# A fused two-block transformer kernel: the first and last Strassen quads get a fifth accumulator, the rms diagonal moves to ScalarE, and constant matmuls run first

## The chip, the cores and the metric

The kernel runs on one core of one Trainium2 chip. The metric is the device time of one launch in microseconds (us); several runs are made and the median is given. The core has TensorE (PE, the matrix engine), VectorE (DVE), ScalarE (ACT), GpSimd (POOL) and SyncE (SP); here POOL and SP also start the DMA transfers that bring weights from HBM.

## The reference, cut to what matters

The input is one sequence of 512 positions, 1024 channels wide, in float32. Two blocks follow each other:

```
h = x + mix(rms_norm(x))                       # gated linear attention and latent attention
h = h + square(relu(rms_norm(h) @ w_up)) @ w_down            # mlp, 4096 wide
h = h + (p @ w_ple_proj) * sigmoid(rms_norm(h) @ w_gate + b) # ple
...
for i in range(2):                              # second block
    x = x + (pool_mixer if i == 0 else chunk_attention)(rms_norm(x))
    n = rms_norm(x)
    a = causal_dwconv3(n @ w_gate)              # 2816 wide
    x = x + (silu(a) * (n @ w_val)) @ w_out     # ffn
```

`rms_norm` divides each position by the root of its mean square. All weights are used once, so they stream from HBM through the core. The change touches the mlp and the two ffn stages (their up-projections), the row scales of the norms, and the first microseconds.

## The kernel before, in words

**Layout.** Activations lie transposed: a tile is 128 channels by 512 positions. Every float32 matrix product is made of three matmuls on a high and a low part of each operand (`mm3`: high by high, high by low, low by high), so every weight tile `ws` is split into `wh` (on ACT, a copy that rounds) and `wl` (on DVE, the difference), two halves of 128x512 each.

**Stages and quads.** The stages are mix, mlp, ple, pool, ffn0, att, ffn1. The up-projections of mlp and the ffns use a Strassen-Winograd scheme: after a first group of plain tiles (`first_tiles`, accumulators `pf`), the output tiles are taken in fours, a *quad*, with 7 products in place of 8. `PHASES` lists the seven: b11, b21, n3, n2, n1, b22, t4. In the list of orders they are numbers 0 to 6 in the order of `PHASES`. Each is 24 matmuls into one accumulator bank: b11, n2, n1 and b22 all go into `pq0`, one on top of the other; b21 into `pq1`, n3 into `pq2`, t4 into `pq3`. Intermediate states of `pq0` are wanted, so `quad_step` copies it on ACT after b11 (to `c1`), after n2 (to `u2`) and after n1 (to `u4`); the next phase into `pq0` waits for that copy. DVE then forms the four results (`c1`+`pq1`, `u2`, `u4`, `pq0`), and `quad_row` multiplies them by the row scale `R` into tiles `qr`. `finish` turns these into the inputs of the down-projection: in ffn the convolution and silu (`fb`, on ACT and DVE), the product, and the split into `yh` (ACT) and `yl` (DVE). The down-projection's accumulators are `pdn`; DVE adds them into the residual `x`.

**Weight sums.** n3, n2 and b22 use sums of weight blocks. One tile, called "sum", is loaded by SP with block 0; POOL then adds blocks to it with accumulating DMAs: block 2 at once (for n3), block 3 after n3's split (for n2), block 1 after n2's split (for b22). `LOADS` says when in the stream of work units each tile is asked for. The tile called "low", for n1, takes one such DMA too.

**Row scale.** `stats` sums the squares with PE (`pst`), takes the power on POOL (`r`), multiplies the identity by `r` on DVE (`dg`, four tiles of 128x128), sums the columns on PE (`psr`), and copies that on ACT to `R`.

**What sets the order.** The program is written out by a planner, and the scheduling is manual: the order in which the planner issues instructions is the order in each engine's stream. Tasks (`spawn`) have priorities; `drive` issues the best task whose inputs are ready on a modelled clock (`Pace.note`), and `splitter` keeps the weight splits up to `lazy` units ahead of their use, with `NW` = 4 buffers each for `wh` and `wl`.

In the trace nearly every instruction carries line 147, the helper that records and issues; the functions themselves are `stats` (line 497), `mix_start` (554), `units_quads` (1242), `quads` (1297) and `quad_step` (1342).

Of the kernel before, what the change touches and what calls it, by code (L numbers as in the profile page):

```python
# [12 lines left out]
AF = mybir.ActivationFunctionType  # L13
OP = mybir.AluOpType
# [36 lines left out]
PHASES = (("b11", 0, True, "a11"), ("b21", 1, True, "a12"), ("n3", 2, True, "sum"), ("n2", 0, False, "sum"),  # L51
          ("n1", 0, False, "low"), ("b22", 0, False, "sum"), ("t4", 3, True, "a22"))

ORDERS = (0, 1, 2, 3, 6, 4, 5), (2, 0, 1, 3, 6, 4, 5)

LOADS = (("sum", 0, -3, (2,)), ("a11", 0, 1, ()), ("a12", 1, 2, ()), ("low", 2, 2.5, (3,)), ("a22", 3, 4, ()))

# [119 lines left out]
class Quad:  # L177


    def __init__(self, src):  # L180
        self.src, self.tile = src, {}


class Block:
# [86 lines left out]
    def plan_loads(self):  # L271

        self.loads, known = [], set()
        for n, u in enumerate(self.units):
            if not isinstance(u[0], str):
                self.loads.append((n, n, u[0], u[1], None, ()))
            elif u[1] not in known:
                known.add(u[1])
                for name, block, at, more in LOADS:
                    self.loads.append((n + at, u[1], u[1].src[block], 1024, name, more))  # L280
        self.loads.sort(key=lambda e: e[0])

# [214 lines left out]
    def stats(self, norm, row):  # L497
        nc = self.nc
        late = 0.0 if norm.gain == self.GAIN["mix"] else self.LATE
        self.pace.ready[norm.acc.tensor.name] += late  # L500
        yield self.room(7)
        yield [norm.acc]
        ps = self.bank("pst")
        for j in range(NT):
            nc.tensor.matmul(ps[:, j:j + 1], norm.acc[:, j * P:(j + 1) * P], self.ones[:, :1], start=True, stop=True,
                             skip_group_check=True)
        norm.acc = None
        norm.ms = self.small("ms", NT)
        nc.vector.tensor_scalar(norm.ms, ps[:, :NT], 1.0 / DM, EPS, op0=OP.mult, op1=OP.add)
        self.free()  # L510
        norm.r = self.power("r", norm.ms, NT)
        if not row:
            return
        yield [norm.r]
        dg = self.slot("dg")
        for j in range(NT):
            nc.vector.tensor_scalar(dg[:, j * P:(j + 1) * P], self.ident, norm.r[:, j:j + 1], None, op0=OP.mult)
        self.pace.ready[dg.tensor.name] += late
        yield self.room(7)
        yield [dg]  # L520
# [33 lines left out]
    def mix_start(self, norm):  # L554
# [9 lines left out]
        def split(d):  # L564
            norm.xs[d] = self.hilo("xs", xin[d], scale=self.col(norm.gain, d))

        load(0)
        load(1)
        self.load_units(1)
# [671 lines left out]
    @staticmethod  # L1241
    def units_quads(plain, src, downs, sizes):

        quads, units, order, wait = [Quad(src[4 * i:4 * i + 4]) for i in range(sum(sizes) - 1)], [], [], []
        q, left = -1, sum(sizes)
        for g, n in enumerate(sizes):
            for i in range(n):
                left -= 1
                if q < 0:
                    order.append((q, 0))  # L1250
                    units += plain
                else:
                    most = 0 if q == 0 else -(-len(wait) // (n - i)) if left else len(wait) - 2
                    for at, ph in enumerate(ORDERS[q > 0]):
                        order.append((q, ph))
                        units.append(("quad", quads[q], ph))
                        for _ in range(((5, 2, 6, 3) if i else (5, 6, 4, 3))[:min(most, len(wait))].count(at)):
                            order.append(wait[0][:2])
                            units.append(wait.pop(0)[2])
                q += 1  # L1260
            for w in wait:
                order.append(w[:2])
                units.append(w[2])
            wait = [("down", (g, u), x) for u, x in enumerate(downs[g])]
        for w in wait:
            order.append(w[:2])
            units.append(w[2])
        return units, order

    def first_tiles(self, norm, take, acts):  # L1270

# [22 lines left out]
            if w % 2:  # L1294
                self.spawn(self.finish(acts, rows, w // 2, 0), -1)

    def quads(self, norm, order, sizes, last, after, take, finish, late=None):


        group = []  # L1300
# [5 lines left out]
        for what, i in order:  # L1306
# [4 lines left out]
            if what < 0:  # L1311
                yield from self.first_tiles(norm, take, acts[0])
                continue
            block, acc, first, _ = PHASES[i]
            if quad is None:
                if late is not None and what == sum(sizes) - 2:
                    self.spawn(late(), 5)
                ps, quad = [None] * 4, {"norm": norm, "take": take, "rows": [None, None], "left": [2, 2],
                                        "acts": acts[group[what + 1]], "at": what + 1 - group.index(group[what + 1])}
            yield from self.unit(8, P)  # L1320
            unit = self.got
# [13 lines left out]
                             first and k == 0 and w == 0, k == 3)  # L1335
            self.used(ps[acc])
            if i != 2:
                self.spawn(self.quad_step(i, ps, quad), -3)
            if i == 5:
                ps = quad = None  # L1340

    def quad_step(self, i, ps, quad):

        s, v = self.nc.scalar, self.nc.vector
        yield [ps[PHASES[i][1]]]
        if i in (0, 3, 4):
            name = {0: "c1", 3: "u2", 4: "u4"}[i]
            t = self.slot(name)
# [2 lines left out]
        if i == 3:  # L1351
            yield [t, ps[2]]
            v.tensor_sub(t, ps[2], t)
        elif i == 1:
            yield lambda: "c1" in quad
            t = quad["c1"]
            yield [t]
            v.tensor_add(t, ps[1], t)
            self.free()
            self.spawn(self.quad_row(quad, 0, 0, t), -2)  # L1360
        elif i == 4:
            yield [t, ps[2]]
# [41 lines left out]
    def units_mlp(self):  # L1404
        a = self.a
        at, downs = 0, []
        for n in QG1:
            downs.append([(a["w_down"][at + i], 1024) for i in range(4 * n)])
            at += 4 * n
        units, self.order["mlp"] = self.units_quads([(a["w_up0"][i], 1024) for i in range(4)],  # L1410
                                                    [a["w_up"][i] for i in range(FF1 // P - 4)], downs, QG1)
        return units

    def mlp(self, norm, after):
# [13 lines left out]
                self.sub(l, z, h.bitcast(F32))  # L1428
                acts[4 * i + 2 * r + w] = h, l

        yield from self.quads(norm, self.order["mlp"], QG1, 4, after, take, finish, self.load_p)
        norm.blocks = None

    def product(self, norm, name, finish):
# [141 lines left out]
    def units_ffn(self, L):  # L1576
        a = self.a
        at, downs = 0, []
        for n in QG2:
            downs.append([(a[f"w_fo{L}"][at + i], 1024) for i in range(2 * n)])  # L1580
            at += 2 * n
        units, self.order["ffn", L] = self.units_quads([(a[f"w_f{L}_0"][i], 1024) for i in range(4)],
                                                       [a[f"w_f{L}"][i] for i in range(2 * FF2 // P - 4)], downs, QG2)
        return units

    def ffn(self, L, norm, after):
# [27 lines left out]
                acts[2 * i + w] = self.hilo("y", y)  # L1614

        gates = {}
        yield from self.quads(norm, self.order["ffn", L], QG2, 2, after, self.mul, finish)
        norm.blocks = None


# [344 lines left out]
```

## Time and profile before

| | |
|---|---|
| median of 3 runs | 1682.46 us (1681.58 to 1685.93) |
| the profiled execution's own time | 1680.26 us |
| its span, first to last instruction | 1678.5 us |
| PE busy | 1626.3 us, 97% of the span |
| DVE busy | 1262.8 us, 75% |
| ACT busy | 882.0 us, 53% |
| POOL busy | 282.4 us, 17% |
| mean granted TensorE clock | 0.992 |

How to read it: the span is what the trace covers; the time of the execution holds 1.8 us more. The profiled execution is 2.2 us under the median of the three runs. A PE that is busy 97% of the span leaves about 52 us of gaps; what a change of this kind can win or lose lies in these gaps and in the stretches where the clock stands below 1.

### The profile page before, as it was taken

To read this page: it belongs to the slowest core of one execution; us is meant where nothing else is said; L and a number is where in the kernel's file an instruction comes from. 1 tells how busy PE (TensorE), PEld (TensorE's weight loads), DVE (VectorE), ACT (ScalarE), POOL (GpSimd) and SP (SyncE) were. 2 spreads that over 40 slices of the span, in tenths; PEclk is the share of its full clock that TensorE was granted. 3 is DMA by queue.
4 is the path that set the end of the run, shared out by engine and by line. 5 is a ranking of instruction groups with operands and counts; after the bars stand their busy time and mean duration, and the time that the engine had idled before them with its cause. 6 is when DMAs were issued, how large, how long until landed. Compare 5 with 4: busy or idle time off the path is not lost. (4 is left out here: it accounts for less than half of the span.)

```text
span 1678.5 us, 27783 instructions
## 1 busy us (share of the span) xinstructions
PE 1626.3 (97%) x10640; PEld 1459.2 (87%) x10640; DVE 1262.8 (75%) x2444; ACT 882.0 (53%) x1714; POOL 282.4 (17%) x312
## 2 busy tenths in 40 slices
PE   8999999999999999989999999999999989999998
PEld 6878778799999988879999998999998879999997
DVE  6986778766666667878787778576678988787776
ACT  6746446544444455845454444476656654454542
POOL 3441302000000013211111100322222211011100
PEclk9999999999999999989999999999999999999999
DMA  7101233566566423267777763322122367776751
GB/s 266 63 26 39 77 100 90 150 163 163 163 164 174 140 101 116 63 164 179 185 191 186 190 163 126 114 76 89 64 92 73 103 161 189 188 189 183 180 156 60
DMA packets 66390, 224.85 MB, mean 134 GB/s; under 512 B 7617, under 2 KB 9554, under 8 KB 66258
## 3 DMA queue, kind: packets, MB, share of 16 engines
q1 hardware_dynamic: 50706, 166.46, 28.1%
q0 software_dynamic: 15552, 56.63, 19.1%
q8 instruction: 83, 1.36, 0.3%
q14 instruction: 49, 0.40, 0.1%
HBM read 220.96 MB, written 2.10 MB: 133 GB/s over the span
## 5 line engine op out<-in xcount | busy, mean ns | idle before, releaser
L147 ACT ACTIVATE wh<-ws 128x512 fp32r<-128x512 f32 x690 | 392.8, 621 | 257.9 <-PE pdn L147 121.5
L147 DVE TENSOR_TENSOR wl<-ws,wh 128x512 fp32r<-128x512 f32 x665 | 437.0, 699 | 91.0 <-ACT wh L147 90.8
L147 PE MATMUL pq<-xsh,wh 128*128 128x256 f32 x864 | 246.6, 285 | 10.1 <-ACT u L147 10.1
L147 PE MATMUL pq<-xsl,wh 128*128 128x256 f32 x864 | 245.8, 285 | 0.0
L147 PE MATMUL pq<-xsh,wl 128*128 128x256 f32 x864 | 245.8, 284 | 0.0
L147 PEld LDWEIGHTS pq<-xsh,wh 128*128 128x128 f32 x864 | 167.1, 193 | 12.9 <-ACT u L147 11.7
L147 DVE TENSOR_TENSOR x<-x,pdn 128x512 f32<-128x512 f32 x177 | 119.8, 680 | 74.8 <-PE pdn L147 74.7
L147 POOL DMA_DIRECT2D ws<-in_w_f x80 | 70.7, 936 | 593.6 <-DVE wl L147 309.2
L147 PEld LDWEIGHTS pq<-xsl,wh 128*128 128x128 f32 x864 | 167.2, 193 | 1.2
L147 PEld LDWEIGHTS pq<-xsh,wl 128*128 128x128 f32 x864 | 167.0, 193 | 0.0
L147 PE MATMUL pdn<-yl,wh 128*128 128x512 f32 x352 | 138.7, 394 | 3.0 <-DVE yl L147 3.0
L147 PE MATMUL pdn<-yh,wh 128*128 128x512 f32 x352 | 138.2, 392 | 1.1 <-ACT yh L147 1.1
L147 PE MATMUL pdn<-yh,wl 128*128 128x512 f32 x352 | 137.5, 391 | 0.0
L147 PE MATMUL pq<-xch,wh 128*128 128x256 f32 x432 | 126.0, 292 | 7.1 <-ACT wh L147 5.3
L147 PE MATMUL pq<-xch,wl 128*128 128x256 f32 x432 | 124.5, 288 | 1.0 <-DVE wl L147 1.0
L147 PE MATMUL pq<-xcl,wh 128*128 128x256 f32 x432 | 123.9, 287 | 0.0
L147 PE MATMUL paq<-wh,xsh 128*128 128x256 f32 x384 | 111.3, 290 | 1.8 <-DVE akk L147 1.2
L147 PE MATMUL paq<-wl,xsh 128*128 128x256 f32 x384 | 108.6, 283 | 0.0
L147 PE MATMUL paq<-wh,xsl 128*128 128x256 f32 x384 | 108.5, 283 | 0.0
L147 PE MATMUL pdn<-hh,wh 128*128 128x512 f32 x256 | 99.9, 390 | 0.0
L147 PE MATMUL pdn<-hl,wh 128*128 128x512 f32 x256 | 99.9, 390 | 0.0
L147 PE MATMUL pdn<-hh,wl 128*128 128x512 f32 x256 | 99.6, 389 | 0.0
(328 smaller groups left out, 3914.8 us busy)
## 6 DMA issues: line engine op xcount, KB each, us to landing
ws<-in_w_f SPq DMA_DIRECT2D x108, 512.0 KB, 4.3
ws<-in_w_f POOLq DMA_DIRECT2D x80, 512.0 KB, 5.4
ws<-in_w_fo SPq DMA_DIRECT2D x44, 512.0 KB, 5.1
ws<-in_w_up SPq DMA_DIRECT2D x39, 512.0 KB, 3.3
ws<-in_w_down SPq DMA_DIRECT2D x32, 512.0 KB, 3.7
ws<-in_w_up POOLq DMA_DIRECT2D x28, 512.0 KB, 5.6
ws<-in_w_out SPq DMA_DIRECT2D x8, 512.0 KB, 3.2
ws<-in_w_gate SPq DMA_DIRECT2D x8, 512.0 KB, 3.2
```

The lines of the kernel that those rows point to most:

```text
L147: return call(*args, **kw)
```

## The change

- The three orders are now called FIRST (0,1,2,3,6,4,5: the order the first quad of a stage had before), MOST (2,0,1,3,6,4,5: as before) and LAST (2,0,1,3,5,4,6: new, with b22 ahead of n1 and t4 at the end). LAST is used for the last quad of ffn0 and of ffn1. mlp's last quad keeps MOST.
- In quads with FIRST (mlp, ffn0, ffn1) or LAST (ffn0, ffn1), b22 starts a fifth accumulator `pq4` of its own; DVE adds it to `u4`, and the fourth result gets its own slot `c22`.
- In a first quad the "sum" tile is asked for five units ahead of its use, not three.
- The diagonal `dg` is made on ACT instead of DVE in all stages but mix, and the planner is told to expect it later (1.5 times the allowance), so it places `psr` later.
- Ahead of everything, 18 matmuls of constant tiles, `warm`, 128x128 in float32.

```diff
-ORDERS = (0, 1, 2, 3, 6, 4, 5), (2, 0, 1, 3, 6, 4, 5)
+FIRST, MOST, LAST = (0, 1, 2, 3, 6, 4, 5), (2, 0, 1, 3, 6, 4, 5), (2, 0, 1, 3, 5, 4, 6)
...
                 for name, block, at, more in LOADS:
+                    at = -5 if u[1].order == FIRST and name == "sum" else at
...
-            nc.vector.tensor_scalar(dg[:, j * P:(j + 1) * P], self.ident, norm.r[:, j:j + 1], None, op0=OP.mult)
-        self.pace.ready[dg.tensor.name] += late
+            if late:
+                nc.scalar.activation(dg[:, j * P:(j + 1) * P], self.ident, AF.Copy, scale=norm.r[:, j:j + 1])
+            else:
+                nc.vector.tensor_scalar(dg[:, j * P:(j + 1) * P], self.ident, norm.r[:, j:j + 1], None, op0=OP.mult)
+        self.pace.ready[dg.tensor.name] += 1.5 * late
...
+        ps = self.bank("warm")
+        for _ in range(18):
+            self.tc.nc.tensor.matmul(ps[:, :P], self.ones, self.ones, start=True, stop=True)
+        self.free()
         load(0)
...
-                    for at, ph in enumerate(ORDERS[q > 0]):
+                    quads[q].order = FIRST if q == 0 else MOST if left or most > 0 else LAST
+                    for at, ph in enumerate(quads[q].order):
...
+            own = quads[what].order != MOST
+            if i == 5 and own:
+                acc, first = 4, True
...
-            if i == 5:
+            if i == quads[what].order[-1]:
                 ps = quad = None
...
         elif i == 4:
             yield [t, ps[2]]
-            v.tensor_sub(t, ps[2], t)
+            c = self.slot("c22") if own else t
+            v.tensor_sub(c, ps[2], t)
+            self.free(2 if own else 1)
+            quad["c22"] = True
+            self.spawn(self.quad_row(quad, 1, 1, c), -2)
+        elif i == 5 and own:
+            yield lambda: "c22" in quad
+            t = quad["u4"]
+            yield [t, ps[4]]
+            v.tensor_add(t, ps[4], t)
             self.free()
-            self.spawn(self.quad_row(quad, 1, 1, t), -2)
+            self.spawn(self.quad_row(quad, 0, 1, t), -2)
```

**How the order moves, 1: ACT in the last quad of ffn0.** `wh_10592` before and `wh_10617` now are n2's split, `wh_10705` and `wh_10654` are b22's (both read the "sum" tile, `ws_10138` and `ws_10163`), `c1` and `u2` are the copies of `pq0`. Before:

```order
L147 ACTIVATE wh_10592<-ws_10138 128x512 x2
L147 ACTIVATE yh_10602<-qr_10380 128x512
L147 ACTIVATE wh_10629<-ws_10371 128x512 x2
L147 ACTIVATE c1_10640<-pq0_10591 128x512
L147 ACTIVATE yh_10642<-qr_10381 128x512
L147 ACTIVATE wh_10667<-ws_10336 128x512 x2
L147 ACTIVATE wh_10705<-ws_10138 128x512 x2
L147 ACTIVATE u2_10716<-pq0_10591 128x512
```

Now:

```order
L148 ACTIVATE wh_10617<-ws_10163 128x512 x2
L148 ACTIVATE yh_10627<-qr_10405 128x512
L148 ACTIVATE wh_10654<-ws_10163 128x512 x2
L148 ACTIVATE c1_10665<-pq0_10616 128x512
L148 ACTIVATE yh_10667<-qr_10406 128x512
L148 ACTIVATE wh_10692<-ws_10361 128x512 x2
L148 ACTIVATE wh_10730<-ws_10396 128x512 x2
L148 ACTIVATE u2_10741<-pq0_10616 128x512
```

b22's split, which waits for the third addition to the "sum" tile, stood behind the `c1` copy and now stands ahead of it. In the last quad of ffn1 the same rows move in the same way.

**How the order moves, 2: DVE in the first quad of ffn0.** `dg` is the diagonal, `c1` the first result, `qr` from `pf` the plain tiles' scaling by `R`, `qr` from `c1` the first result's; the three pairs of `wl` are the splits of n2, t4 and n1. Before:

```order
L147 TENSOR_SCALAR dg_7484<-ident_65,r_7431 128x128 x4
L147 TENSOR_TENSOR c1_7492<-pq1_7483,c1_7492 128x512
L147 TENSOR_TENSOR qr_7439<-pf_7204,R_7525 128x512
L147 TENSOR_TENSOR qr_7440<-pf_7205,R_7525 128x512
L147 TENSOR_TENSOR qr_7441<-pf_7206,R_7525 128x512
L147 TENSOR_TENSOR qr_7442<-pf_7207,R_7525 128x512
L147 TENSOR_TENSOR qr_7540<-c1_7492,R_7525 128x256
L147 TENSOR_TENSOR qr_7541<-c1_7492,R_7525 128x256
L147 TENSOR_TENSOR wl_7554<-ws_6713,wh_7553 128x512 x2
L147 TENSOR_TENSOR wl_7561<-ws_7031,wh_7560 128x512 x2
L147 TENSOR_TENSOR wl_7569<-ws_6954,wh_7568 128x512 x2
```

Now:

```order
L148 TENSOR_TENSOR c1_7514<-pq1_7505,c1_7514 128x512
L148 TENSOR_TENSOR wl_7568<-ws_6653,wh_7567 128x512 x2
L148 TENSOR_TENSOR wl_7575<-ws_7053,wh_7574 128x512 x2
L148 TENSOR_TENSOR wl_7583<-ws_6976,wh_7582 128x512 x2
L148 TENSOR_TENSOR qr_7461<-pf_7226,R_7559 128x512
L148 TENSOR_TENSOR qr_7462<-pf_7227,R_7559 128x512
L148 TENSOR_TENSOR qr_7463<-pf_7228,R_7559 128x512
L148 TENSOR_TENSOR qr_7464<-pf_7229,R_7559 128x512
L148 TENSOR_TENSOR qr_7594<-c1_7514,R_7559 128x256
L148 TENSOR_TENSOR qr_7595<-c1_7514,R_7559 128x256
L148 TENSOR_TENSOR u2_7626<-pq2_7537,u2_7626 128x512
```

The diagonal has left DVE, and the six scalings now follow the six weight splits that they preceded. The first quad of ffn1 shows the same exchange.

## Rows read from the trace of the kernel before

**Rows 1.** Waits of PE: engine, who released it: total us, times, longest.

```profile
PE pq L147 <- ACT u L147: 10.1, 8, 2.1
...
PE pq L147 <- ACT wh L147: 5.3, 3, 3.3
```

**Rows 2.** Timeline of the start, PE and DVE: start, us, engine, operation, [idle before].

```profile
7.84 0.80 PE L147 MATMUL pl<-xsh,wh 128*128 128x512 f32 x1 [7.84 <-ACT wh L147]
...
11.85 0.45 PE L147 MATMUL pl<-xsh,wh 128*128 128x512 f32 x1
...
9.03 4.06 DVE L147 SCALAR_TENSOR_TENSOR xsl<-xin,cols,xsh 128x512 fp32r<-128x512 f32 x6
```

**Rows 3.** Timeline of PE, first quad of mlp: n1, then b22.

```profile
306.65 0.38 PE L147 MATMUL pq<-xsh,wh 128*128 128x256 f32 x1 [1.98 <-ACT u L147]
...
310.47 0.38 PE L147 MATMUL pq<-xsh,wh 128*128 128x256 f32 x1 [0.69 <-ACT u L147]
```

**Rows 4.** Timeline of PE, first quad of ffn0: psr, n2, n1, b22, down-projection.

```profile
721.65 1.78 PE L147 MATMUL psr<-dg,ones 128*128 128x512 f32 x2 [2.21 <-DVE dg L147]
...
727.90 0.39 PE L147 MATMUL pq<-xch,wh 128*128 128x256 f32 x1 [1.44 <-ACT wh L147]
...
736.70 0.39 PE L147 MATMUL pq<-xsh,wh 128*128 128x256 f32 x1 [0.78 <-ACT u L147]
...
741.90 0.39 PE L147 MATMUL pq<-xsh,wh 128*128 128x256 f32 x1 [2.07 <-ACT u L147]
...
755.71 0.40 PE L147 MATMUL pdn<-yh,wh 128*128 128x512 f32 x1
```

**Rows 5.** Busy time by stretch, ffn0: PE, PEld, DVE, ACT, POOL, granted clock, DMA.

```profile
741.90:745.60 3.70, 3.70 (x19) 3.70 (x20) 3.67 (x8) 1.67 (x3) 0.53 (x1) 0.57 0.95 164
```

**Rows 6.** Timeline of POOL, ACT, DVE, first quad of ffn0.

```profile
720.26 1.32 POOL L147 DMA_DIRECT2D ws<-in_w_f  x1
...
727.22 3.23 ACT L147 ACTIVATE wh<-ws 128x512 fp32r<-128x512 f32 x6 [3.16 <-DMA ws<-in_w_f]
...
724.09 2.48 DVE L147 TENSOR_TENSOR qr<-pf,R 128x512 f32<-128x512 f32 x4 [1.99 <-ACT R L147]
726.49 0.75 DVE L147 TENSOR_TENSOR qr<-c,R 128x256 f32<-128x256 f32 x2
727.88 3.70 DVE L147 TENSOR_TENSOR wl<-ws,wh 128x512 fp32r<-128x512 f32 x6 [0.64 <-ACT wh L147]
731.50 1.53 DVE L147 SCALAR_TENSOR_TENSOR fb<-qr,cols,fb 128x511 f32<-128x511 f32 x2
```

**Rows 7.** Timeline of PE, first quad of ffn1: n2, n1, b22, down-projection.

```profile
1349.27 0.39 PE L147 MATMUL pq<-xch,wh 128*128 128x256 f32 x1 [3.29 <-ACT wh L147]
...
1358.37 0.39 PE L147 MATMUL pq<-xsh,wh 128*128 128x256 f32 x1 [1.10 <-ACT u L147]
...
1363.58 0.56 PE L147 MATMUL pq<-xsh,wh 128*128 128x256 f32 x1 [2.08 <-ACT u L147]
...
1377.40 0.40 PE L147 MATMUL pdn<-yh,wh 128*128 128x512 f32 x1
```

**Rows 8.** Timeline of POOL, ACT, PE, last quad of ffn0: b22's addition, c1, b22's split, n2.

```profile
1011.87 0.86 POOL L147 DMA_DIRECT2D ws<-in_w_f  x1 [12.30 <-DVE wl L147]
...
1013.33 0.60 ACT L147 ACTIVATE c<-pq 128x512 f32<-128x512 f32 x1 [1.26 <-PE pq L147]
...
1017.09 1.15 ACT L147 ACTIVATE wh<-ws 128x512 fp32r<-128x512 f32 x2 [1.60 <-DMA ws<-in_w_f]
...
1016.01 0.28 PE L147 MATMUL pq<-xch,wh 128*128 128x256 f32 x1
```

**Rows 9.** Timeline of PE, end of ffn0: b22, down-projection.

```profile
1025.50 0.38 PE L147 MATMUL pq<-xsh,wh 128*128 128x256 f32 x1 [0.69 <-ACT u L147]
...
1028.47 0.40 PE L147 MATMUL pdn<-yh,wh 128*128 128x512 f32 x1
...
1043.17 0.80 PE L147 MATMUL pdn<-yl,wh 128*128 128x512 f32 x1 [1.84 <-DVE yl L147]
```

More of the change, by code (lines that the diff above doesn't have):

```diff
@@ L180, in __init__ @@
     def __init__(self, src):
-        self.src, self.tile = src, {}
+        self.src, self.tile, self.order = src, {}, MOST
 class Block:
@@ L1267, in units_quads @@
             units.append(w[2])
-        return units, order
+        return units, order, quads
     def first_tiles(self, norm, take, acts):
@@ L1295, in first_out, with quads @@
                 self.spawn(self.finish(acts, rows, w // 2, 0), -1)
-    def quads(self, norm, order, sizes, last, after, take, finish, late=None):
+    def quads(self, norm, order, quads, sizes, last, after, take, finish, late=None):
         group = []
@@ L1317, in quads @@
                     self.spawn(late(), 5)
-                ps, quad = [None] * 4, {"norm": norm, "take": take, "rows": [None, None], "left": [2, 2],
+                ps, quad = [None] * 5, {"norm": norm, "take": take, "rows": [None, None], "left": [2, 2],
                                         "acts": acts[group[what + 1]], "at": what + 1 - group.index(group[what + 1])}
@@ L1337, in quads, with quad_step @@
             if i != 2:
-                self.spawn(self.quad_step(i, ps, quad), -3)
-            if i == 5:
+                self.spawn(self.quad_step(i, ps, quad, own), -3)
+            if i == quads[what].order[-1]:
                 ps = quad = None
-    def quad_step(self, i, ps, quad):
+    def quad_step(self, i, ps, quad, own):
         s, v = self.nc.scalar, self.nc.vector
-        yield [ps[PHASES[i][1]]]
+        yield [ps[4 if i == 5 and own else PHASES[i][1]]]
         if i in (0, 3, 4):
@@ L1409, in units_mlp @@
             at += 4 * n
-        units, self.order["mlp"] = self.units_quads([(a["w_up0"][i], 1024) for i in range(4)],
+        units, *self.order["mlp"] = self.units_quads([(a["w_up0"][i], 1024) for i in range(4)],
                                                     [a["w_up"][i] for i in range(FF1 // P - 4)], downs, QG1)
@@ L1429, in finish @@
                 acts[4 * i + 2 * r + w] = h, l
-        yield from self.quads(norm, self.order["mlp"], QG1, 4, after, take, finish, self.load_p)
+        yield from self.quads(norm, *self.order["mlp"], QG1, 4, after, take, finish, self.load_p)
         norm.blocks = None
@@ L1581, in units_ffn @@
             at += 2 * n
-        units, self.order["ffn", L] = self.units_quads([(a[f"w_f{L}_0"][i], 1024) for i in range(4)],
+        units, *self.order["ffn", L] = self.units_quads([(a[f"w_f{L}_0"][i], 1024) for i in range(4)],
                                                        [a[f"w_f{L}"][i] for i in range(2 * FF2 // P - 4)], downs, QG2)
@@ L1616, in ffn @@
         gates = {}
-        yield from self.quads(norm, self.order["ffn", L], QG2, 2, after, self.mul, finish)
+        yield from self.quads(norm, *self.order["ffn", L], QG2, 2, after, self.mul, finish)
         norm.blocks = None
```

## The prediction

> **What bounds the kernel now.** I read the page first: PE is busy for 97% of the span, so the time is PE's busy time plus its gaps, and a cut in another engine's work pays only where that engine ends a gap. The table of PE's waits comes next [rows 1]: the two largest that this change aims at are the copies `c1`/`u2`/`u4` on ACT (10.1 us in 8 waits) and splits on ACT (5.3 us in 3). Then the timelines around these waits. In the first quad of ffn0 [rows 4] the reader sees four stops: 2.21 us before `psr`, 1.44 before n2, 0.78 before n1, 2.07 before b22. After a long stop the granted clock is at the lower level, 1.2 GHz: the 3.70 us behind the 2.07 us stop were at 0.57 of full speed [rows 5], so they hold 3.70 x 0.43 = 1.6 us of loss. I use 1.6 as the price of every stop of 2.07 us or more; behind the stop of 1.98 us [rows 3] I charge none, since n1 there takes 3.1 us (306.65 to 310.47 less 0.69), as long as n1 in ffn0 (736.70 to 741.90 less 2.07 [rows 4]).
>
> **The change part by part**, against the profiled execution's 1680.3 us.
>
> *Warm matmuls.* PE stands idle up to 7.84, then runs at the lower level: the first matmul takes 0.80 us and from 11.85 on they take 0.45 and less [rows 2]. That is 4.0 us at half speed, 2.0 us lost. PE cannot win all of it, because the left operands come from DVE: its six xsl take 4.06 us from 9.03, so the last is ready at 13.1, and I see room for 1.7. Price of the added work: `psr` is the same kind of product with 512 columns and takes 1.78 us at the lower level [rows 4]; 128 columns are a quarter, 0.44 us, or 0.22 at the upper one. 18 from about 1 us on end at 8.9 if all are slow, which delays the first matmul by 1.1; with 9 slow ones (4 us, as long as the stretch after 7.84) and 9 fast ones at 7.0, a gap of 0.9 that no row shows to lower the clock. I take **-1.7**, ends -2.0 and +1.1.
>
> *First quad of mlp.* n1 waits 1.98 us for `u2`, b22 0.69 for `u4` [rows 3]. b22 goes to its own bank, and in ACT's new order `u2` stands ahead of b22's split. Both go: **-2.7**, ends -2.7 and 0 if the down-projection's inputs, which come from DVE and ACT, are then late instead.
>
> *First quad of ffn0.* The diagonal on ACT removes the reason of the 2.21 us stop, and `psr` is placed later among n3's matmuls. But n2 gains nothing: its split on ACT waits for the addition that POOL issues at 720.26, and starts at 727.22 after 3.16 us of idling on that DMA [rows 6]. POOL issues in the same order after the change (the earlier load of "sum" does not move the second addition, which follows n3's split and `r`), so n2 starts at 727.9 as before and its stop takes up what `psr` gave. From there PE saves 0.78 + 2.07 and the 1.6 of clock: 4.5 us at the end of b22. That does not last, since DVE gives it back. Before, DVE did four `qr` from 724.09 and two from 726.49, while it had nothing else to do, and only then the six `wl` from 727.88 [rows 6]. Now the six scalings stand behind the six `wl`, and DVE has no pause. From 727.88 to the second `yl` of the first group its new order has 33 operations of 128x512 (20 `wl`, 6 `qr`, 5 sums of accumulators, 2 `yl`), 10 `qr` of 128x256 and 8 `fb`. By the starts of rows 6 a 128x512 takes (731.50 - 727.88)/6 = 0.60 us; the others 0.75/2 = 0.37 and 1.53/2 = 0.77. 33 x 0.60 + 10 x 0.37 + 8 x 0.77 = 29.7 us, so the second `yl` is there at 757.6. Before, the matmul that takes its place in the order began at 755.71 [rows 4]. PE arrives some 4.5 us early, stands for long and pays the clock again: +1.9 and 1.6, so **+3.5**, ends +1.9 (no loss of clock) and +4.1 (DVE waits for b21 of the next quad as well).
>
> *First quad of ffn1.* The same. n2 starts at 1349.27 [rows 7] with DVE's first `wl`; the list has two `wl` fewer, 28.5 us, so the second `yl` comes at 1377.8 where PE needed it at 1377.40: +0.4 and 1.6, **+2.0**, ends +0.4 and +2.7. What it saves ahead of that (1.10, 2.08, 1.6) is swallowed.
>
> *Last quad of ffn0.* LAST puts b22 right behind n2, so its split moves up in ACT's order, ahead of the `c1` copy (the first order piece). That split waits for the third addition to "sum": POOL issues it at 1011.87, and ACT, idle for 1.60 us on it, starts the split at 1017.09 [rows 8]. The issue stays where it is, since it follows n2's `wl`. So `c1`, which ran at 1013.33, now comes behind two halves of a split, 1.15 us: it runs at 1018.2 and ends at 1018.8. n2, which began at 1016.01 without a wait [rows 8], must have that copy: a new stop of **2.8 us**, and 1.6 of clock behind it. The wait for `u4` before b22 (0.69, [rows 9]) goes. After the quad the down-projection starts, before at 1028.47; its second half waited for the last `yl` until 1043.17 [rows 9], 14.7 us on. In DVE's new order I count between these points the same six `wl`, eight residual sums, four `fb`, six scalings and two `yl` as before, and one `u2` sum more (t4 is now the last phase), with four scalings of other results just ahead: +0.6 to +1.5, I take +1.1. Sum 2.8 + 1.6 - 0.7 + 1.1 = **+4.8**, ends +3.8 and +5.5.
>
> A rule for the same transfer: the Trainium skill, "DMA: Bandwidth & Descriptors" (section "Anatomy of one DMA — SWDGE (gpsimd) path"), fits a transfer issued by GpSimd as about 2.0 us plus its bytes at 436 GB/s: for 512 KB an estimate of 3.2 us, where the rows show 5.2. By that rule b22's split would start at 1015.1, the new stop would be 0.9 us without a loss of clock, and each last quad would cost 3.5 us less (the whole sum +4). The row is this very transfer, so it decides.
>
> *Last quad of ffn1.* The same rows of ACT move; I take the same, **+4.8**, ends +3.8 and +7 (its end runs at full clock now and may lose it).
>
> *Elsewhere.* `psr` later in ple and the exchanges that the planner makes in the attention's tail: 0, ends -1 and +1. No row there shows a queue that they are moved behind.
>
> Sum: -1.7 - 2.7 + 3.5 + 2.0 + 4.8 + 4.8 = **+10.7**, that is 1691.0 on the profiled execution, which stands 2.2 us under the median of the runs shown (1682.5). On the median it would be 1693.2; I say 1692. A difference under 0.3% (5 us) cannot be told from none here.
>
> **The rivals.**
>
> *It does what it looks made for.* DVE keeps up and ACT is not held at `c1`. Then -1.7 - 2.7, first quads -4.5 and -4.8 (1.10 + 2.08 + 1.6), last quads -0.7 each, and the stop of 1.84 us at the end of ffn0 shrinks with its clock (-3.4): about -18, **1664**. For it: each of these waits stands in the rows. Against it: the two order pieces, which show no slack at either place. Chance 0.12.
>
> *Only the last quads bind.* DVE's list is shorter than I count, or PE reaches the down-projection later: -1.7 - 2.7 - 4.5 - 4.8 + 9.6 = -4.1, **1678**. It decides at DVE's pace: 4 us less than 29.7 and PE no longer waits. Chance 0.18, half of it below -5 us.
>
> *Only DVE binds.* The addition lands earlier than 5.2 us after its issue, for instance because fewer transfers run beside it: -4.4 + 5.5 and the last quads between -0.7 and +0.4: about +1, **1683**. It decides at a landing before 1013.3. Chance 0.15.
>
> *Both bind* (the forecast): chance 0.55, 1687 to 1697 by the ends of the terms.
>
> **How the numbers follow.** The forecast is slower by over 5 us but for about 0.03 of its chance. Faster: 0.12 + 0.09 = 0.21. Same: 0.09 + 0.13 + 0.03 = 0.25. Slower: the rest, 0.54. The range of 1674 to 1697 leaves out the first rival and the ends; the likeliest case alone has 1687 to 1697.
>
> **What would show each step.** Right: PE stops of 2 us or more before n2 in both last quads, released by ACT's `c` and not by a split; PE stops before the first down-projection of ffn0 and ffn1, released by DVE `yl`, with DVE busy throughout from 727.9; no wait on `u` in any first quad; matmuls at full speed from the first weight on. Wrong: if n2 in the last quads starts without a wait, the addition came sooner or `c1` was not held, and 9 us of my sum go; if the first down-projections start some 4 us earlier than 755 and 1377, DVE was not the bound and 14 us go; if n2 in the first quad of ffn0 starts well before 727.9, the earlier load did move the second addition.

## The result and the profile after

The changed kernel takes 1702.0 us (median of 4 runs, 1700.45 to 1705.17), the kernel before 1683.8 us in the runs beside it (1681.58 to 1685.93). The ratio is 1.0111, 95% interval 1.0089 to 1.0133: slower by 1.1%, or 18 us, where 10 were forecast. The profiled execution has a span of 1698.7 us against 1678.5, 20.2 us more, and these 20.2 us can be laid out place by place. The page of the changed kernel first:

```profile
span 1698.7 us, 27854 instructions
...
PE 1638.1 (96%) x10676; PEld 1467.1 (86%) x10676; DVE 1260.0 (74%) x2435; ACT 887.4 (52%) x1730; POOL 280.1 (16%) x310
```

PE's busy time has grown by 11.8 us. 6.0 of them are the constant matmuls (36 records, two for each), in time in which PE stood idle before; the other 5.8 are the same matmuls taking longer, at a lower clock. What remains of the 20.2 us, 14.4, are longer stops. The waits of PE in the changed kernel (engine, who released it: total us, times, longest):

```profile
PE pdn L148 <- ACT yh L148: 14.7, 5, 7.2
PE pq L148 <- ACT wh L148: 9.6, 3, 4.2
PE pdn L148 <- DVE yl L148: 5.6, 5, 1.8
PE pq L148 <- ACT c L148: 5.6, 2, 2.8
...
PE psr L148 <- ACT dg L148: 1.5, 1, 1.5
```

The waits on `u` that the change aimed at, 10.1 us in [rows 1], are gone from the list. In their place stand waits of the down-projection on `yh` and `yl`, and two waits on `c`. The timeline of PE shows where:

```profile
7.83 0.50 PE L148 MATMUL pl<-xsh,wh 128*128 128x512 f32 x1 [0.79 <-ACT wh L148]
...
719.08 0.70 PE L148 MATMUL psr<-dg,ones 128*128 128x512 f32 x1 [1.46 <-ACT dg L148]
...
724.50 0.39 PE L148 MATMUL pq<-xch,wh 128*128 128x256 f32 x1 [3.58 <-ACT wh L148]
...
753.98 0.79 PE L148 MATMUL pdn<-yh,wh 128*128 128x512 f32 x1 [7.25 <-ACT yh L148]
...
756.04 0.80 PE L148 MATMUL pdn<-yl,wh 128*128 128x512 f32 x1 [1.26 <-DVE yl L148]
...
758.69 0.79 PE L148 MATMUL pdn<-yl,wh 128*128 128x512 f32 x1 [0.59 <-DVE yl L148]
...
1022.08 0.58 PE L148 MATMUL pq<-xch,wh 128*128 128x256 f32 x1 [2.74 <-ACT c L148]
...
1047.24 0.50 PE L148 MATMUL pdn<-yh,wh 128*128 128x512 f32 x1 [1.11 <-ACT yh L148]
...
1049.58 0.79 PE L148 MATMUL pdn<-yl,wh 128*128 128x512 f32 x1 [1.83 <-DVE yl L148]
...
1358.26 0.58 PE L148 MATMUL pq<-xch,wh 128*128 128x256 f32 x1 [4.18 <-ACT wh L148]
...
1385.67 0.80 PE L148 MATMUL pdn<-yh,wh 128*128 128x512 f32 x1 [4.71 <-ACT yh L148]
...
1653.52 0.58 PE L148 MATMUL pq<-xch,wh 128*128 128x256 f32 x1 [2.84 <-ACT c L148]
```

Against [rows 4]: `psr` and n2 of ffn0's first quad come 2.6 and 3.4 us earlier than before, the stops before n1 and b22 are gone, and then PE stands for 7.25 us before the first down-projection. Against [rows 8]: n2 of the last quad of ffn0, which began without a wait, stands for 2.74 us on `c`; ffn1's for 2.84.

The table lays out the difference by stretches, measured between the starts of the same matmuls in the two traces. A first quad's stretch runs from the first matmul of the plain tiles (`pf`; in ffn0 from where they resume after the sums of squares) to a down-projection from which on the two traces repeat the same pattern (every 62.16 us in the ffns). A last quad's stretch runs from the down-projection before it to its own; the end runs from there to the next stage or to the end of the kernel.

| stretch | before, us | after, us | difference | predicted |
|---|---|---|---|---|
| start, to `pw` of mix | 203.62 | 203.28 | -0.3 | -1.7 |
| mlp's first quad | 82.05 | 79.83 | -2.2 | -2.7 |
| ffn0's first quad | 147.01 | 153.44 | +6.4 | +3.5 |
| ffn0's last quad | 107.98 | 111.40 | +3.4 | +4.8 with the end |
| ffn0's end | 26.22 | 28.63 | +2.4 | (in the row above) |
| ffn1's first quad | 167.32 | 171.14 | +3.8 | +2.0 |
| ffn1's last quad | 107.97 | 111.52 | +3.6 | +4.8 with the end |
| ffn1's end | 27.80 | 32.17 | +4.4 | (in the row above) |
| all else | | | -1.3 | 0 |
| span | 1678.5 | 1698.7 | +20.2 | +10.7 |

Every sign that was forecast is right. The sizes are not: the start won less, and the first quads and the ends lost more.

**The last quads.** POOL and ACT in the last quad of ffn0 of the changed kernel, timeline:

```profile
1015.04 0.86 POOL L148 DMA_DIRECT2D ws<-in_w_f  x1 [12.30 <-DVE wl L148]
...
1020.39 1.15 ACT L148 ACTIVATE wh<-ws 128x512 fp32r<-128x512 f32 x2 [6.18 <-DMA ws<-in_w_f]
1021.45 0.58 ACT L148 ACTIVATE c<-pq 128x512 f32<-128x512 f32 x1
```

Compare [rows 8]: there ACT copied `c1` first and then idled 1.60 us for the addition; now it idles 6.18 us for it with the copy queued behind. From POOL's issue to the split are 5.4 us. 2.74 us of stop were forecast as 2.8. The fit of the Trainium skill's page "DMA: Bandwidth & Descriptors" (section "Anatomy of one DMA — SWDGE (gpsimd) path") makes an estimate of 3.2 us for 512 KB. The page does not agree with this transfer, and the row decides.

**The clock.** Busy time by stretch in the changed kernel (PE, PEld, DVE, ACT, POOL, granted clock, DMA share, GB/s): n2 of ffn0's last quad, the end of ffn0, n2 of ffn1's last quad, the end of ffn1.

```profile
1022.00:1026.00 4.00, 3.92 (x21) 3.93 (x22) 3.74 (x8) 2.62 (x6) 0.00 (x0) 0.60 0.51 156
...
1049.50:1055.70 6.20, 6.08 (x13) 4.06 (x14) 3.07 (x6) 1.88 (x3) 0.00 (x0) 0.50 0.22 82
1653.50:1657.00 3.50, 3.48 (x17) 3.48 (x18) 3.24 (x7) 2.57 (x5) 0.00 (x0) 0.54 0.01 2
1681.00:1687.20 6.20, 6.09 (x14) 4.49 (x15) 2.06 (x3) 0.06 (x1) 0.00 (x0) 0.50 0.12 45
```

And the same for the kernel before, at the ends of ffn0 and ffn1:

```profile
1043.10:1046.00 2.90, 2.83 (x7) 2.25 (x8) 0.79 (x3) 0.84 (x2) 0.00 (x0) 0.50 0.42 162
1663.00:1669.00 6.00, 5.30 (x22) 4.18 (x23) 3.21 (x5) 0.01 (x1) 0.00 (x0) 1.00 0.23 87
```

Behind the stops of 2.7 and 2.8 us the loss is 4.0 x 0.40 and 3.5 x 0.46, 1.6 us each, as priced. At the ends it is not: 6.2 us at 0.50 are 3.1 us, where the kernel before lost 2.9 x 0.50 = 1.5 at ffn0's end and nothing in this stretch of ffn1's.

**The first quad of ffn0.** ACT and DVE between b22 and the second `yl`, timeline of the changed kernel:

```profile
743.89 0.60 ACT L148 ACTIVATE c<-pq 128x512 f32<-128x512 f32 x1 [3.08 <-PE pq L148]
748.91 2.19 ACT L148 ACTIVATE wh<-ws 128x512 fp32r<-128x512 f32 x4 [4.42 <-DMA ws<-in_w_f]
751.00 0.61 ACT L148 ACTIVATE fb<-fb 128x512 f32<-128x512 f32 x1
...
753.30 0.63 ACT L148 ACTIVATE yh<-qr 128x512 fp32r<-128x512 f32 x1 [0.97 <-DVE qr L148]
...
724.48 3.70 DVE L148 TENSOR_TENSOR wl<-ws,wh 128x512 fp32r<-128x512 f32 x6 [4.25 <-ACT wh L148]
728.10 2.48 DVE L148 TENSOR_TENSOR qr<-pf,R 128x512 f32<-128x512 f32 x4
...
749.57 2.50 DVE L148 TENSOR_TENSOR wl<-ws,wh 128x512 fp32r<-128x512 f32 x4 [3.90 <-ACT wh L148]
...
757.95 0.69 DVE L148 TENSOR_TENSOR yl<-qr,yh 128x512 fp32r<-128x512 f32 x1
```

The six scalings do stand behind the six `wl`, as forecast. But DVE is not busy throughout: it pauses 3.90 us at 749.57, because ACT idled 4.42 us on another split that waits for an addition. That split is n2's of the *next* quad, and in ACT's order it now comes ahead of the `fb` and `yh` that PE is about to want. It is the mechanism of the last quads a second time, at a place where the prediction did not have it. POOL issued this addition, with another one, between 738.0 and 739.7, so it took over 9 us here, against 5.4 in the last quad. The 6.4 us of this stretch are all stops: PE's busy time for its 970 matmuls is 139.1 us, before 139.4. In ffn1's first quad, where PE stops for 4.71 us at the same place and ACT idles 2.96 us on such a split, 2.0 of the 3.8 us are stops and the rest is a longer busy time (160.8 us against 159.0).

### The profile page after: what moved, and what is told of

It is laid out like the page before. It is cut to its first block, busy times and chain, and to the rows that moved or that the text cites. A ratio compares the mean times of both kernels' runs of the same rounds, so it can differ in the third digit from the quotient of the medians.

```text
span 1698.7 us, 27854 instructions
## 1 busy us (share of the span) xinstructions
PE 1638.1 (96%) x10676; PEld 1467.1 (86%) x10676; DVE 1260.0 (74%) x2435; ACT 887.4 (52%) x1730; POOL 280.1 (16%) x310
## 5 line engine op out<-in xcount | busy, mean ns | idle before, releaser
L148 PE MATMUL pdn<-yh,wh 128*128 128x512 f32 x352 | 142.9, 406 | 14.8 <-ACT yh L148 14.7
L148 PE MATMUL pdn<-yl,wh 128*128 128x512 f32 x352 | 142.8, 406 | 5.7 <-DVE yl L148 5.6
L148 PEld LDWEIGHTS pq<-xch,wh 128*128 128x128 f32 x432 | 85.8, 199 | 18.1 <-ACT wh L148 10.8
```

The lines of the kernel that those rows point to most:

```text
L148: return call(*args, **kw)
```

## Experiments

The theory after the result, A: ACT works its list in order, and the change moves splits that wait for POOL's additions ahead of small operations on PE's path (`c1` in the last quads, `fb` and `yh` of the first group). Rivals: B, the order LAST itself lengthens the end; C, DVE's own list, as I had predicted; D, the fifth accumulator draws the splits forward, whatever DVE does. All ratios are to runs of the kernel before on the same chip.

**LAST undone** (last_undone).

```diff
-                    quads[q].order = FIRST if q == 0 else MOST if left or most > 0 else LAST
+                    quads[q].order = FIRST if q == 0 else MOST
```

> The change with the last quads of ffn0 and ffn1 put back to the order MOST and four accumulators. If all of what the two ends lost (5.8 us in ffn0, 7.9 us in ffn1 between the two traces) comes from LAST, this takes 1702 - 13.7 = 1688 us, with no wait on c1 before n2. If part of it was carried in from the stages ahead (the clock, a later queue), it stays above 1693.

Measured: 1690.1 us, ratio 1.0041 (1.0027 to 1.0055). Both last quads are back at 107.97 us and the ends at 26.3 and 27.8. So the 13.8 us that the table has for the last quads and the ends come from LAST, its order and its fifth accumulator together (12 us by the medians). 8 us slower than before remain: the first quads of the ffns are as long as in the change (153.6 and 170.8 us), less what mlp won.

**b22's split held back until c1 is copied** (c1_first).

```diff
...
+            u = self.units[n]
+            if isinstance(u[0], str) and u[2] == 5 and u[1].order == LAST:
+                yield lambda: "c1" in u[1].had
...
```

> LAST as it is, but the split of b22 in the last quad is held back until c1 has been copied. Theory A (ACT takes its instructions in order, and the split that waits for POOL's addition keeps c1 from being copied): the stops of 2.7 and 2.8 us before n2 go, with 1.6 us of clock each, so 1702 - 8.8 = 1693 us. Rival B (LAST itself lengthens the end, because t4 is last and DVE has one more sum to do): what is won before n2 is waited for again at the last yl, and the time stays at 1699 or more.

Measured: 1693.3 us, ratio 1.0062 (1.0041 to 1.0083), as theory A had it. ACT in the last quad of ffn0 of this kernel, timeline:

```profile
1016.65 0.60 ACT L148 ACTIVATE c<-pq 128x512 f32<-128x512 f32 x1 [2.30 <-PE pq L148]
...
1020.64 3.24 ACT L148 ACTIVATE wh<-ws 128x512 fp32r<-128x512 f32 x6 [2.88 <-DMA ws<-in_w_f]
```

The copy runs as soon as PE is done, and no wait of PE on `c` is left there. The last quads take 107.04 us, 0.9 less than before the change: what LAST is good for, the missing wait on `u4` (0.69 us [rows 9]), shows here. But B holds too: the ends take 29.4 and 31.2 us, 3.2 and 3.4 more than before. PE at the end of ffn0:

```profile
1030.85 0.40 PE L148 MATMUL pdn<-yh,wh 128*128 128x512 f32 x1
...
1043.42 0.50 PE L148 MATMUL pdn<-yh,wh 128*128 128x512 f32 x1 [1.50 <-ACT yh L148]
...
1045.76 0.54 PE L148 MATMUL pdn<-yl,wh 128*128 128x512 f32 x1 [1.84 <-DVE yl L148]
```

The last `yl` comes 14.9 us after the down-projection began, before 14.7 [rows 9]: t4 is now the phase whose result the last products need, and DVE's list behind it is as long as it was behind b22. So LAST wins 0.9 us of quad, and loses over 3 us at the end, even with the stop removed: the stops of ffn0's end shown here are 1.0 us longer together than before (0.53 and 1.84), and the time at the lower clock is longer (0.54 of full speed over the 5.3 us from 1045.7 on, before 0.50 over 2.9 us).

**n2's split of the second quad held back until the first group's products are made** (yh_first).

```diff
...
+            w = self.units[n]
+            if isinstance(w[0], str) and w[2] == 3:
+                yield lambda: all(x is not None for x in w[1].wait_for)
...
+        if last == 2:
+            quads[1].wait_for = acts[0]
```

> In ffn0 and ffn1 the split of n2 of the second quad, which waits for POOL's addition and on which ACT idles for 4.4 us (ffn0) and 3.0 us (ffn1), is held back until the inputs of the first down-projection are made. Theory A (the same order effect on ACT): the first down-projections start 3 to 4 us earlier, 1702 - 6 = 1696 us. Rival C (my prediction: DVE's own list of 29.7 us is what the down-projection waits for): they start within 1 us of where they did, 1700 us or more.

Measured: 1699.6 us, ratio 1.0102 (1.0080 to 1.0124). By the total alone this looks like rival C; the trace says otherwise. PE in this kernel:

```profile
749.91 0.77 PE L148 MATMUL pdn<-yh,wh 128*128 128x512 f32 x1 [2.11 <-ACT yh L148]
...
754.62 0.80 PE L148 MATMUL pdn<-yl,wh 128*128 128x512 f32 x1 [0.59 <-DVE yl L148]
...
1430.86 0.80 PE L148 MATMUL pdn<-yl,wh 128*128 128x512 f32 x1 [1.92 <-DVE yl L148]
```

The stop of 7.25 us is 2.11, and ffn0's first quad takes 149.3 us: 4.1 of the 6.4 us are back, so theory A holds there. The other 2.3 us are not shown to be DVE's list. From n2 at 725.45 to the `yl` of 754.62 are 29.2 us, close to the 29.7 that I had worked out, but DVE does less in them and waits more. The hold moves four of the 20 `wl` behind this `yl`, and DVE pauses 1.33 us for the next quad's b21, the case of my upper end of +4.1, with the product that `yh` needs queued behind that sum:

```profile
747.91 0.69 DVE L148 TENSOR_TENSOR c<-pq,c 128x512 f32<-128x512 f32 x1 [1.33 <-PE pq L148]
748.52 0.68 DVE L148 TENSOR_TENSOR qr<-qr,fb 128x512 f32<-128x512 f32 x1
...
754.49 2.49 DVE L148 TENSOR_TENSOR wl<-ws,wh 128x512 fp32r<-128x512 f32 x4
```

In ffn1 the gain is given back. The stop of 4.71 us on `yh` falls to 0.2, with one of 2.21 us on `yl` behind it, but the held split is late for the next group, whose down-projection stops for 1.92 us at 1430.86, and the stretch takes 174.2 us, 3.0 more than in the change. The stops add up to no more than there; PE's busy time for the same 1067 matmuls is 164.2 us against 160.8, so what is lost is time at the lower clock.

**Fifth accumulator out of the first quads of the ffns** (first_four).

```diff
-            own = quads[what].order != MOST
+            own = quads[what].order == LAST or quads[what].order == FIRST and last == 4
```

> The change with the fifth accumulator taken out of the first quads of ffn0 and ffn1 alone (mlp's first quad and both last quads keep it). If the early b22 there is what sends the planner's later splits ahead of the yh, the 6.6 and 3.8 us lost in these quads come back and 1702 - 10 = 1692 us follow. If the later psr and the moved diagonal do it, the time stays at 1700 or more.

Measured: 1700.8 us, ratio 1.0108 (1.0085 to 1.0132). ffn0's first quad takes 150.2 us, 3.2 less than in the change; ffn1's 172.5, 1.3 more. The accumulator is part of the loss in ffn0 and not its only cause.

**The planner's allowance for the diagonal put back** (allowance_back), and the same without LAST (allowance_last).

```diff
-        self.pace.ready[dg.tensor.name] += 1.5 * late
+        self.pace.ready[dg.tensor.name] += late
```

> The change with one number put back: the planner's allowance for the diagonal is 1.0, not 1.5 times. The diagonal stays on ACT, all fifth accumulators and LAST stay. On DVE the six scalings of the first quads of ffn0 and ffn1 come ahead of the six weight splits again, as before the change. Theory C (DVE's order, set by that allowance, makes the inputs of the first down-projection late): the 6.6 and 3.8 us lost in these quads go, 1702 - 10 = 1692 us. Rival D (the early b22 of the fifth accumulator makes them late, by the splits that it pulls forward on ACT): 1699 or more.

> As allowance_back, and the last quads of ffn0 and ffn1 in the order MOST with four accumulators. If the two causes are separate and are all that was lost, the time is 1702 - 10 - 12 = 1680 us, 3 us under the kernel before (the mlp quad's 2.2 us and the start). If the fifth accumulator's saving in the first quads of the ffns (4.5 and 4.8 us of PE's stops) then comes through, 1672.

Measured: 1698.3 us, ratio 1.0096 (1.0075 to 1.0116), and 1685.4 us, ratio 1.0017 (1.0005 to 1.0028). DVE's order is back, ffn0's first quad takes 149.2 and 149.1 us (4.2 less), ffn1's 170.2 and 170.1 (1.0 less). mlp loses what it had won, 83.3 and 83.6 us: its wait on `u` is back with the old allowance, in spite of the fifth accumulator. That, and the 5 of 10 us that came back in the first quads, put both runs above their expectations (1692, and 1680 or 1672). PE in allowance_back:

```profile
307.06 0.38 PE L148 MATMUL pq<-xsh,wh 128*128 128x256 f32 x1 [1.94 <-ACT u L148]
...
754.73 0.50 PE L148 MATMUL pdn<-yh,wh 128*128 128x512 f32 x1 [2.09 <-ACT yh L148]
...
757.52 0.80 PE L148 MATMUL pdn<-yl,wh 128*128 128x512 f32 x1 [2.28 <-DVE yl L148]
```

Even with the scalings early, the fifth accumulator's saving in ffn0 (the wait before b22) turns up again as stops before the down-projection. But the allowance does not test theory C alone, since it changes ACT's order with DVE's. The first `yh` now stands ahead of the split of the second quad's n2, and ACT idles on that split for 1.04 us in place of 4.42:

```profile
749.60 0.62 ACT L148 ACTIVATE yh<-qr 128x512 fp32r<-128x512 f32 x1
751.26 2.19 ACT L148 ACTIVATE wh<-ws 128x512 fp32r<-128x512 f32 x4 [1.04 <-DMA ws<-in_w_f]
```

> As allowance_last, and the split of n2 of the second quad is held back until the first down-projection's inputs are made. If ACT still idles on that split ahead of the second yh, this is 2 to 4 us faster than allowance_last; if DVE alone sets the down-projection's start, it is the same within 1 us, or 2 us slower from the stops that the held split leaves in the next group.

allowance_last with the hold of yh_first (allowance_last_yh): 1690.4 us, ratio 1.0042 (1.0024 to 1.0060), 5 us slower than without the hold; it gives back in ffn1 (173.3 us against 170.1) more than it wins. In ffn0's first quad it wins 0.2 us (148.9 against 149.1), where the same hold won 4.1 at the allowance of 1.5. So the 4.1 us of the hold and the 4.2 of the allowance are for the most part the same loss, taken away in two ways; they do not add up, and how much of it DVE's order would cost without ACT's wait is not shown.

**Both put back** (allowance_four): the two diffs above together, LAST and all else as in the change.

> The change with the allowance at 1.0 and four accumulators in the first quads of ffn0 and ffn1 (the diagonal stays on ACT, LAST and the earlier sum load stay). If allowance and accumulator are the two causes in the first quads and add up, ffn0's first quad is as long as before (6.4 us less than in the change) and ffn1's about 3 us shorter, while mlp's u2 wait comes back (+3.5): 1702 - 9.4 + 3.5 = 1696 us. If moving the diagonal to ACT is a cause of its own, 1700.

Measured: 1696.2 us, ratio 1.0067 (1.0043 to 1.0091). This closes a square for ffn0's first quad:

| ffn0's first quad, us | allowance 1.5 | allowance 1.0 |
|---|---|---|
| fifth accumulator | 153.4 (the change) | 149.2 (allowance_back) |
| four accumulators | 150.2 (first_four) | 146.5 (allowance_four) |

The kernel before has 147.0. Accumulator (2.7 to 3.2) and allowance (3.7 to 4.2) add up to all of the loss, and the diagonal on ACT has none of it. Each cell is one trace; the three traces with the first quads of the change lie within 0.2 us of each other, the five with those of the kernel before (two of them with the earlier sum) between 145.9 and 147.0. In ffn1 the square is 171.1, 170.2, 172.5, 168.3 (before: 167.3): 2.9 of the 3.8 us are back with both, but the two do not add up there.

**The planner told when an addition can start** (planner_told).

```diff
+                self.pace.free["gpsimd"] = max(self.pace.free["gpsimd"], self.pace.ready[l.tensor.name])
                 nc.gpsimd.dma_start(t, quad.src[ADDED[ph]], accum_op=OP.add)
```

> The change, and one line more in the planner: POOL's modelled clock for an addition to a weight tile starts only when the DVE split that reads that tile is done, as it does on the chip. If all that goes wrong at the ends is that the planner puts b22's split ahead of c1 because it thinks the addition has landed, the stops before n2 in the last quads go by this line alone and the time is that of c1_first or less: 1693 us at most. If the modelled clock is not what orders them, they stay and so do 1702 us.

Measured: 1690.0 us, ratio 1.0042 (1.0023 to 1.0062), 12 us less than the change by one line. Its ACT copies `c1` of ffn0's last quad ahead of b22's split:

```profile
1014.64 0.60 ACT L148 ACTIVATE c<-pq 128x512 f32<-128x512 f32 x1 [2.30 <-PE pq L148]
...
1018.55 1.15 ACT L148 ACTIVATE wh<-ws 128x512 fp32r<-128x512 f32 x2 [2.79 <-DMA ws<-in_w_f]
```

With that the last quads take 107.04 us, as in c1_first, and the ends 28.3 and 31.1. So at the last quads the cause of the stop lies in the planner's clock: it lets the addition begin before the DVE operation that it must wait for, and puts the split where the sum would be ready on that clock. In the first quads the line changes little (152.2 and 170.8 us).

**The constant matmuls alone** (warm_alone), **the rest of the edit in mlp alone** (mlp_fifth_alone, mlp_part), and the sum's load time (sum_late, mlp_part_sum, mlp_part_told). The diff of mlp_part against the change, with the two diffs of last_undone and first_four:

```diff
-            if late:
+            if late and norm.gain == self.GAIN["mlp"]:
                 nc.scalar.activation(dg[:, j * P:(j + 1) * P], self.ident, AF.Copy, scale=norm.r[:, j:j + 1])
...
-        self.pace.ready[dg.tensor.name] += 1.5 * late
+        self.pace.ready[dg.tensor.name] += (1.5 if norm.gain == self.GAIN["mlp"] else 1.0) * late
```

> The kernel before with the 18 constant matmuls and nothing else. My prediction's step: 1.7 us faster throughout, 1682 us. The trace of the change says: 1.4 to 2 us are won up to 45 us and only 0.3 are left at 93 us, because DVE's chain of the position tables and norms ends at the same time: 1683 us, no difference.

> The kernel before with the constant matmuls, the earlier load of sum and the fifth accumulator in mlp's first quad alone: diagonal on DVE, allowance 1.0, four accumulators in all quads of the ffns, no LAST. The two gains seen in the traces remain: mlp 2.2 us, the start 0.3 to 2.1 us. 1683 - 3 = 1680 us. If the earlier sum load costs something of its own in the ffns, it is 1684 or more.

> The kernel before with the constant matmuls, and all that the change does in mlp's first quad: fifth accumulator, earlier sum, diagonal on ACT, allowance 1.5 there. Everything in the ffns as before (four accumulators, diagonal on DVE, allowance 1.0), no LAST. The trace of the change has mlp 2.2 us shorter and the start 0.3 us: 1683 - 2.5 = 1680.5 us. If the mlp gain needs the ffns' settings too, 1683.

> As mlp_part, with the planner's line of planner_told. If splits that wait on an addition hold back ACT elsewhere too (c1 waits at 787 and 1409 us in the trace before), 1 to 5 us less than mlp_part; if not, the same within 2 us.

> The change with the sum of a first quad asked for three units ahead, as before. If the earlier load pulls the later transfers together and costs in ffn1 (stop before the second quad's n2 at c), 2 to 4 us less than 1702; if it is harmless, 1702; if it does what it is for, n2 of the first quads starts later and the time is 1704 or more.

> As mlp_part, with the earlier sum load in mlp alone. In mlp_part the second quad's n2 in ffn1 waited 3.4 us for c, 1.15 before. If the earlier load is the reason, 2 to 3 us under mlp_part: 1676 us. If it is not, 1678.5.

| run | median, us | ratio (95% interval) |
|---|---|---|
| warm_alone | 1682.7 | 0.9994 (0.9983 to 1.0004) |
| mlp_fifth_alone | 1681.4 | 0.9989 (0.9975 to 1.0002) |
| mlp_part | 1678.6 | 0.9973 (0.9961 to 0.9985) |
| mlp_part_told | 1685.7 | 1.0016 (1.0003 to 1.0028) |
| sum_late | 1703.7 | 1.0115 (1.0089 to 1.0141) |
| mlp_part_sum | 1681.3 | 0.9980 (0.9967 to 0.9993) |

The constant matmuls by themselves are worth nothing that can be told from none: 1.1 us are won at `pst` (27.14 against 28.27) and 0.2 are left at `pw` (203.46 against 203.62), as in the change, where the trace names DVE's `km` as the next to be waited for at 54.66 us:

```profile
54.66 0.44 PE L148 MATMUL pq<-wuh,lath 128*128 128x384 f32 x1 [0.97 <-DVE km L148]
```

mlp_part and mlp_part_sum beat both kernels; mlp_part by 0.27% (0.15 to 0.39) of the kernel before. Where the gain sits is not shown: mlp_part's traced execution took 1683.2 us, 4.6 over its median. In mlp the allowance counts: in all ten traces with 1.5 there the stretch takes 78.6 to 81.6 us, in all seven with 1.0 82.05 to 83.6, mlp_fifth_alone (fifth accumulator, old allowance) among them with 82.5. No run has 1.5 with four accumulators in mlp, so whether the accumulator is needed stays open. Not everything in the ffns of mlp_part is as before, as its expectation has it: the earlier load of the sum is in them too. That load is worth 2 us of ffn1's first quad in the change (173.3 us in sum_late, 171.1 with it; the medians cannot be told apart) and costs in mlp_part (ffn1 170.5 us with it, 167.9 without, in mlp_part_sum), so it has no price of its own; the medians of mlp_part and mlp_part_sum differ by less than their intervals allow to tell. The planner's line, good for 12 us in the change, makes mlp_part slower: a corrected estimate in one place gives another order everywhere, not a better one.

## Why the prediction was right or wrong

- **Slower: right, and for the last quads by the reason given.** The 2.8 us before n2, the loss of 1.6 us of clock behind it and the `u4` wait that goes all came as worked out (3.4 and 3.6 us in the quads against 3.7), and c1_first and planner_told show the cause: the copy queued behind a split that waits for an addition.
- **First quads: the step that failed is "DVE has no pause".** I took DVE's list of 29.7 us from n2 on as the only bound. As work the list is right: in the change it has the 20 `wl` and the rest that I counted, and from 724.48 to the second `yl`'s matmul at 758.69 pass 34.2 us, of which DVE pauses 3.90 at 749.57 and twice 0.5 us before, which leaves 29.4. But the pauses were not in the sum. ACT idles 4.42 us (ffn0) on n2's split of the second quad, ahead of `fb` and `yh`, and DVE pauses with it. I had read ACT's order for this effect in the last quads alone. So the second `yl`'s matmul comes 6.2 us later in its stretch than the matmul in its place before, where I had 1.9. The 1.6 us of clock that I added in ffn0 did not come: PE's busy time there did not grow. yh_first shows that holding this split back returns 4.1 of the 6.4 us. In terms of the edit, allowance and fifth accumulator bear the loss in ffn0, about 4 and 3 us; what DVE's order costs without ACT's wait stays open.
- **The ends of ffn0 and ffn1: mis-sized.** I took +1.1 for the longer chain. It is +2.4 and +4.4. The extra stops are small (1.11 and 1.83 us against 0.53 and 1.84 in ffn0); the clock is the rest, 3.1 us against 1.5 and 0. I had priced the clock once per long stop, and not for the end of ffn1, where I named it only as an upper end. c1_first shows that it comes with LAST and not with the stop before n2.
- **n2 of the first quad of ffn0** was forecast at 727.9 as before; it began at 724.50. That is 16.4 us into its stretch, before 16.6, so the step holds: the 3.3 us won ahead of the stretch carried through, and POOL's addition moved with them (717.39 against 720.26 [rows 6]). That its stop takes up what `psr` wins was right as well: 3.58 against 1.44 us. The stop before `psr` did not go, though: it is 1.46 us, on ACT's `dg`.
- **The start: right to 45 us, wrong as a gain of the kernel.** 1.4 us are won at `pst`, 0.3 remain at 203 us. I had costed the matmuls and not asked who is late next on the way: DVE's `km`.
- **mlp: -2.2 for -2.7.** Both waits on `u` went, but n2's stop grew from 0.54 to 1.82 us. And the reason given was not enough: the fifth accumulator does not remove the wait before n1 without the allowance of 1.5.
- **The rivals and the range.** "It does what it looks made for" had no support; "only the last quads bind" and "only DVE binds" are out as well, since both ends and both first quads lost. The forecast case was right on where the loss is, and right on what causes it in the last quads alone. All four terms of loss went past their own upper ends (6.4 us against 4.1, 3.8 against 2.7, 5.8 against 5.5, 8.0 against 7). The stated top of 1697 counts the upper ends of these four only; with those of the start, mlp and the rest the sum is +21.4, 1704. The mis-sized terms, some 5 us for the first quads and 4 for the last quads with their ends, are what put the time at 1702.

## What to carry to other kernels

Where engines work their lists in order, a move that frees one engine is to be followed on the lists of the others over the next whole unit of work, not only at the place edited: a cheap operation that PE needs is late by what is left of the wait of the split ahead of it. A bound worked out from one engine's list holds only if no item of the list waits, directly or through another engine, for a DMA. And an order made on a modelled clock is only as good as that model's waits: one missing dependence (the addition behind the reading split) cost 12 us here, while putting it right in another variant made that one slower, so each variant has to be timed.

## What the runs showed of the hardware

The constant matmuls end at 7.0 us, as estimated with half of them slow: PE works on 14 of their 36 records from 1 to 4 us and on 24 from 4 to 7.1 (the two at the border are in both). The first weights then meet a PE at full speed: between 7.80 and 11.80 us it does 16 matmuls, in the kernel before 9, with a stop of 0.79 us ahead of them that costs no clock. The granted clock reads 1.00 in these stretches of both kernels, so the level is read from the matmuls themselves:

```profile
7.80:11.80 4.00, 3.96 (x9) 3.13 (x10) 3.98 (x7) 4.00 (x7) 0.00 (x0) 1.00 1.06 406
...
7.80:11.80 4.00, 3.97 (x16) 2.73 (x16) 3.99 (x7) 4.00 (x7) 0.00 (x0) 1.00 1.06 408
```

The first line is the kernel before, the second the changed one. What a stop costs in clock is not always the same: 0.60 of full speed over 4.0 us and 0.54 over 3.5 us behind the stops of the last quads, 0.50 over 6.2 us at the ends. Why the ends cost more is open: in the kernel before, ffn0's end had two stops as well (0.53 and 1.84 us) and 0.50 over 2.9 us. A stop of about 2 us goes either way: behind the one of 1.94 us in allowance_back the granted clock falls,

```profile
307.00:311.40 4.40, 4.34 (x24) 4.34 (x25) 4.17 (x8) 2.61 (x6) 0.00 (x0) 0.62 0.46 149
```

and behind the one of 1.98 us in the kernel before [rows 3] it does not:

```profile
306.60:310.40 3.80, 3.13 (x24) 2.93 (x24) 3.57 (x7) 3.18 (x7) 0.00 (x0) 1.00 0.51 155
```

It is the same phase with the same 24 matmuls, 1.2 us longer in the first. So the price of 1.6 us from 2.07 us on, and none at 1.98, does not mark a line: a shorter stop cost 1.2.
